# Two heads in turn in the third layer's half-array products, with one ring of six PSUM banks

## The chip, the core and the metric

The kernel runs on one core of a Trainium2 chip. The metric is the device time of one execution in microseconds (us); the time before is the median of three runs.

## The reference, cut to what matters

Three layers work in turn on 512 tokens of width 1024: a gated delta-rule layer, a stick-breaking attention layer, and a third layer with two branches and a mixture of experts ("PEER"). All is float32. The change concerns two stages of the third layer, and an ordering in the second. The third layer's windowed attention has 16 query heads of 64 dimensions, 2 key and value heads, blocks of 128 queries that each see their own block and the one before, and a sink logit a head:

```python
s = jnp.einsum('bqhgd,bkhd->bhgqk', qj, kj) * scale
s = jnp.where(valid, s, -jnp.inf)
m = jnp.maximum(jnp.max(s, axis=-1, keepdims=True), sink)
p = jnp.exp(s - m)
denom = jnp.sum(p, axis=-1, keepdims=True) + jnp.exp(sink - m)
return jnp.einsum('bhgqk,bkhd->bqhgd', (p / denom), vj)
```

Its second branch is a matrix-memory recurrence (mLSTM) of 8 heads with keys of 64 and values of 128 dimensions; within a block it needs the scores `einsum('bhtd,bhsd->bhts', qj, kj) * w_intra`.

## The kernel before, in words

TensorE (PE) does all products; a product is a weight load (the stationary operand) and a matmul that streams the other operand past it. Activations and weights of the projections are split into a high and a low part, so that three one-pass products stand for one (`mm3`, lines 104 to 108); the attention's own products are plain float32, and the trace shows each of them as two records. A head has 64 dimensions, so two heads lie in the two halves of the 128 partitions. Their score products use 64 rows of the array, their value products 64 columns of it.

The program is written in one order of source lines. A scheduler then places the instructions on the engines' queues: on each engine it takes what is ready by its own timing, earlier source lines first as a rule, so that projections of later steps fill the time in which PE would wait. Nothing is pinned by hand in the stages that change, apart from the dependences. PSUM has eight banks; two serve projections (`pj`), the other six are shared out by tags (`psum`, `pg`).

`window_pair` (lines 877 to 931) does one pair of heads in the third layer, 8 calls, each in two steps (`t2`) of two query blocks. For each head `e` it writes the mask into a bank of tag `l` by a product with the identity (line 895, full array, 256 columns) and adds the scores (line 896, 64 rows, 256 columns, 128 for the first block), block after block, so that full-array and half-array products alternate. VectorE (DVE) takes the maximum (898), ScalarE (ACT) the exponential with its sum (906), DVE scales (916), PE transposes into the bank `pt` (918), DVE or ACT copies (922), and PE multiplies with the values (928, 64 columns) into the bank `x`, first all of head 0, then all of head 1. Banks: three `l`, one each `x`, `t` (the transposes of the query norm, line 713) and `pt`.

`mlstm_pair` (lines 1001 to 1085), 4 calls, makes for each of two heads the decay matrix `W` (1030, 1032) and the scores (1035, four products of 64 rows and 128 columns) and multiplies them (1037). Its banks are two `w`, three `num`, one `pc`.

`sb_pair` (lines 775 to 820) is the second layer's attention, 8 calls. There the source lists scores (790) and value products (819) with the two heads in turn already, on six banks of one tag.

Of the kernel before, what the change touches and what calls it, by code (L numbers as in the profile page):

```python
# [2 lines left out]

# [1 line left out]

# [5 lines left out]
F32 = mybir.dt.float32  # L11
# [4 lines left out]
AF = mybir.ActivationFunctionType  # L16
ALU = mybir.AluOpType
AX = mybir.AxisListType

P = 128  # L20
# [3 lines left out]
NT = T // P  # L24
# [9 lines left out]
class Net:  # L34
# [185 lines left out]
        self.split(H[:, k], L[:, k], n, eb=nc.gpsimd if k % 2 else nc.vector)  # L220


    def wtile(self, w, j0, n=2, ks=slice(0, KC)):


        nc = self.nc
        self.uid += 1
        raws = []
        for j in range(n):
            raw = self.wr.tile([P, KC, P], F32, tag="raw", name=f"wr{self.uid}_{j}")  # L230
            nc.sync.dma_start(raw[:, ks], w[j0 + j][:, ks])
            raws.append(raw)
        parts = {}

        def at(k):
            f = k // self.part
            if f not in parts:
                fs = slice(max(f * self.part, ks.start), min((f + 1) * self.part, ks.stop))
                wh = self.ws.tile([P, self.blocks, self.part, P], F32R, tag="wh", name=f"wh{self.uid}")
                wl = self.ws.tile([P, self.blocks, self.part, P], F32R, tag="wl", name=f"wl{self.uid}")  # L240
                o = slice(fs.start - f * self.part, fs.stop - f * self.part)
                for j, raw in enumerate(raws):
                    self.split(wh[:, j, o], wl[:, j, o], raw[:, fs], eb=nc.gpsimd if self.uid % 9 else nc.vector)
                parts[f] = wh, wl
            wh, wl = parts[f]
            return wh[:, :n, k % self.part], wl[:, :n, k % self.part]
        return at
# [79 lines left out]
class Gdn(Net):  # L327
    SPARE_SB, SPARE_2, SPARE_P = "pj pj l l", "pj pj l l", "pj pj s s"
    RAW, SB_, PART = 3, 3, 2
    FIRST, OFF, A0, WB, SPARE_0, SQ = (0, 8, 16), (), 12, 6, "v0", 8  # L330
    SP = 5
    YB = 8
    EARLY_A, EARLY_OUT = (slice(0, 7), slice(7, 8)), (slice(0, 6), slice(6, 8))
    RATE, LV = 1.0, 100
# [342 lines left out]
class Sb(Gdn):  # L677
# [97 lines left out]
    def sb_pair(self, wk, j, kT, qT, v, idr, sbm, nui, nones):  # L775


        nc = self.nc
        mm = nc.tensor.matmul
        half = [slice(e * 64, e * 64 + 64) for e in range(2)]  # L780

        names = ("b0", "b1", "c0", "c1", "a0", "a1")
        bank = {n: self.pg()[:, :256 if n < "d" and n > "c" else T] for n in names}

        def reg(t, e, b):
            o = 384 if b == 3 else 0
            return t[f"{'abcb'[b]}{e}"][:, o:o + (NT - b) * P]
        order = [(e, b) for b in (1, 3, 2, 0) for e in range(2)]
        for e, b in order:
            mm(reg(bank, e, b), kT[half[e], b * P:(b + 1) * P], qT[half[e], b * P:],  # L790
               start=b != 3, stop=False, skip_group_check=True)
        for e, b in order:
            mm(reg(bank, e, b)[:, :P], idr, sbm, start=False, stop=True, skip_group_check=True)
        sH, sL, wt = {}, {}, {}
# [9 lines left out]
        for n in names:  # L804
            e = int(n[1])
# [7 lines left out]
                            bufs=2 if n[0] == "c" else self.SP)  # L813
            nc.scalar.activation(wt[n], bank[n], AF.Exp)
        po = self.pg()
        for b in range(NT):
            for e in range(2):
                h = 2 * j + e
                mm(po[half[e], b * P:], v[:, b, h * 64:(h + 1) * 64], reg(wt, e, b), start=b == 0, stop=b == NT - 1)
        return po  # L820


# [4 lines left out]
class Second(Sb):  # L827
# [49 lines left out]
    def window_pair(self, wk, j, qT, kTx, v, wmask, idr, aH, aL):  # L877

        nc = self.nc
        mm = nc.tensor.matmul  # L880
        kv = j // 4
        po = self.pg("x")
        sink = self.col("sink", 2 * j, 2).unsqueeze(1).to_broadcast([P, 2, 2])
        for t2 in range(0, NT, 2):
            small = lambda n: wk.tile([P, 2, 2], F32, tag=n, name=f"{n}{j}_{t2}", bufs=3)
            mx, den, sm = small("mx"), small("den"), small("sm")
            lg = []
            for e in range(2):
                L = self.pg("l").rearrange("p (i s) -> p i s", i=2)
                lg.append(L)  # L890
                pr = slice(e * 64, e * 64 + 64)
                for i in range(2):
                    tb = t2 + i
                    n = P if tb == 0 else 2 * P
                    mm(L[:, i], idr, wmask[tb > 0], start=True, stop=False)
                    mm(L[:, i, 2 * P - n:], qT[pr, tb * P:(tb + 1) * P], kTx[e == kv][pr, (tb + 1) * P - n:(tb + 1) * P],
                       start=False, stop=True)
                nc.vector.tensor_reduce(mx[:, :, e], L, axis=AX.X, op=ALU.max)
            nc.vector.tensor_tensor(mx, mx, sink, op=ALU.max)
            nc.vector.tensor_tensor(den, sink, mx, op=ALU.subtract)  # L900
            nc.vector.tensor_scalar(mx, mx, -1.0, None, op0=ALU.mult)
# [4 lines left out]
                    nc.scalar.activation(Pm[e][:, i], lg[e][:, i], AF.Exp, bias=mx[:, i, e:e + 1], accum_out=sm[:, i, e:e + 1])  # L906
            nc.vector.tensor_tensor(den, den, sm, op=ALU.add)
            nc.vector.reciprocal(den, den)
            for e in range(2):
                pr = slice(e * 64, e * 64 + 64)  # L910
                pT = self.pg("pt")
                k = 0
                for i in range(2):
                    n = min(t2 + i + 1, 2)
                    x = Pm[e][:, i, (2 - n) * P:]
                    nc.vector.tensor_scalar(x, x, den[:, i, e:e + 1], None, op0=ALU.mult)
                    for b in range(n):
                        nc.tensor.transpose(pT[:, k * P:(k + 1) * P], x[:, b * P:(b + 1) * P], self.ident)
                        k += 1
                PT = wk.tile([P, 4, P], F32, tag="PT", name=f"PT{j}_{e}_{t2}")  # L920
                ev = nc.scalar.copy if e else nc.vector.tensor_copy
                ev(PT[:, :k], pT[:, :k * P].rearrange("p (k t) -> p k t", t=P))
                k = 0
                for i in range(2):
                    tb = t2 + i
                    n = min(tb + 1, 2)
                    for b in range(n):
                        mm(po[pr, tb * P:(tb + 1) * P], v[:, tb + 1 - n + b, kv * 64:kv * 64 + 64], PT[:, k],
                           start=b == 0, stop=b == n - 1)
                        k += 1  # L930
        self.split(aH[:, j], aL[:, j], po)

# [68 lines left out]
    def mlstm_pair(self, wk, j, qT, kT, mv, gcol, rr, selp, dcm, mo, hH, hL):  # L1001

        nc = self.nc
# [14 lines left out]
        for i in range(NT):  # L1018
# [1 line left out]
        kw = new("mkw", [NT, 2, 64])  # L1020
        nc.vector.tensor_tensor(kw, p.rearrange("p (i e d) -> p i e d", i=NT, e=2),
                                gcol[:, 1, :, 2 * j:2 * j + 2].unsqueeze(3).to_broadcast([P, NT, 2, 64]), op=ALU.mult)
        PT = {}
        for e in range(2):
            h = 2 * j + e
            pr = slice(e * 64, e * 64 + 64)
            pm = self.rep(h, rr)
            W = new("mW", [NT, P])
            for i in range(NT):
                nc.vector.scalar_tensor_tensor(W[:, i], pm[:, i * P:(i + 1) * P], gcol[:, 0, i, h:h + 1], dcm,  # L1030
                                               op0=ALU.add, op1=ALU.add)
            nc.scalar.activation(W, W, AF.Exp)
            p = self.pg()
            for i in range(NT):
                mm(p[:, i * P:(i + 1) * P], kT[pr, i * P:(i + 1) * P], qT[pr, i * P:(i + 1) * P], start=True, stop=True)
            PT[e] = new("mPT", [NT, P], 3)
            nc.vector.tensor_tensor(PT[e], v4(p), W, op=ALU.mult)

        num = [self.pg("num")[:, :3 * (P + 1)].rearrange("p (g c) -> p g c", c=P + 1) for _ in range(3)]
        at = lambda i, e: num[(2 * i + e) // 3][:, (2 * i + e) % 3]  # L1040
# [46 lines left out]
    def second(self, x):  # L1087
        nc, tc, a = self.nc, self.tc, self.a
        w = a["w_in"]
        with ExitStack() as st:  # L1090
# [18 lines left out]
                self.proj_T(w, 10 + j2, 2, act, lambda j, p: keep("mq", j2 + j, p, 1.0))  # L1109
                self.proj_T(w, 14 + j2, 2, act, lambda j, p: keep("mk", j2 + j, p, 0.125))  # L1110
            with ExitStack() as s1:
                self.TT = "t"
                self.psum(s1, l=3, x=1, t=1, pt=1)
                wk = s1.enter_context(tc.tile_pool(name="c_wk", bufs=2))
                c1 = s1.enter_context(tc.tile_pool(name="c_c1", bufs=1))
                idr, wp, wc = self.load_const(c1, ("id", "wp", "wc"), F32R)
# [523 lines left out]
```

## Time and profile before

| | |
|---|---|
| median of three runs | 2853.34 us (2845.3 to 2853.7) |
| the profiled execution | 2852.8 us, span 2851.0 us |
| PE busy | 2671.3 us, 94% of the span |
| DVE busy | 1786.9 us, 63% |
| ACT busy | 1210.9 us, 42% |
| POOL busy | 1765.5 us, 62% |
| mean granted TensorE clock | 0.98 |

The span is the time from the first to the last instruction of the profiled execution, and its own time lies just around it. Engines run beside each other, so their shares don't add up. PE is the matmul stream, PEld its weight loads. Matmuls are pipelined: a record's duration reaches over the start of the next one, and what a product costs is read from one start to the next. In the rows below, `64*128 64x256` is a product that uses 64 rows and 128 columns of the array and streams 256 columns; `x8` joins eight records.

### The profile page before, as it was taken

To read this page: it belongs to the slowest core of one execution; us is meant where nothing else is said; L and a number is where in the kernel's file an instruction comes from. 1 tells how busy PE (TensorE), PEld (TensorE's weight loads), DVE (VectorE), ACT (ScalarE), POOL (GpSimd) and SP (SyncE) were. 2 spreads that over 40 slices of the span, in tenths; PEclk is the share of its full clock that TensorE was granted. 3 is DMA by queue.
4 is the path that set the end of the run, shared out by engine and by line. 5 is a ranking of instruction groups with operands and counts; after the bars stand their busy time and mean duration, and the time that the engine had idled before them with its cause. 6 is when DMAs were issued, how large, how long until landed. Compare 5 with 4: busy or idle time off the path is not lost. (4 is left out here: it accounts for less than half of the span.)

```text
span 2851.0 us, 40457 instructions
## 1 busy us (share of the span) xinstructions
PE 2671.3 (94%) x14601; PEld 2266.0 (79%) x14601; DVE 1786.9 (63%) x3095; ACT 1210.9 (42%) x2508; POOL 1765.5 (62%) x1335
## 2 busy tenths in 40 slices
PE   6999898799998999999998989998998999999999
PEld 4877777697776877778786988898998978877777
DVE  7767664614446654122332989899899166778886
ACT  5566663636654454233333333333333333333332
POOL 4889883533333522433463468788788378888786
PEclk9999999899998999999999999999999999999999
DMA  6334331221011111221222587887987879999996
GB/s 240 108 119 125 111 113 31 76 90 60 31 39 54 56 45 60 74 69 66 69 79 89 160 296 261 284 290 256 314 277 281 276 272 344 340 333 331 333 328 227
DMA packets 206793, 499.35 MB, mean 175 GB/s; under 512 B 18304, under 2 KB 106624, under 8 KB 203520
## 3 DMA queue, kind: packets, MB, share of 16 engines
q1 hardware_dynamic: 167856, 359.19, 37.6%
q0 software_dynamic: 36864, 134.23, 13.1%
q10 hardware_dynamic: 1872, 3.33, 0.4%
q8 instruction: 115, 1.88, 0.3%
q14 instruction: 86, 0.70, 0.1%
HBM read 444.26 MB, written 52.43 MB: 174 GB/s over the span
## 5 line engine op out<-in xcount | busy, mean ns | idle before, releaser
L102 POOL TENSOR_TENSOR wl<-wr,wh 128x256 fp32r<-128x256 f32 (+2 forms) x499 | 414.8, 850 | 499.2 <-ACT wh L99 468.5
L102 POOL TENSOR_TENSOR upl<-upr,uph 128x1024 fp32r<-128x1024 f32 x128 | 312.9, 2445 | 97.0 <-ACT uph L99 96.3
L99 ACT ACTIVATE wh<-wr 128x256 fp32r<-128x256 f32 (+2 forms) x556 | 228.7, 445 | 302.6 <-PE pj L107 120.4
L106 PE MATMUL pj<-nH,downh 128*128 128x384 f32 x1024 | 354.3, 346 | 2.3 <-ACT w L1459 1.7
L108 PE MATMUL pj<-nH,downl 128*128 128x384 f32 x1024 | 349.6, 341 | 4.6 <-DVE downl L102 4.6
L107 PE MATMUL pj<-nL,downh 128*128 128x384 f32 x1024 | 348.8, 341 | 0.0
L102 POOL TENSOR_TENSOR downl<-downr,downh 128x1024 fp32r<-128x1024 f32 x96 | 243.9, 2542 | 129.3 <-ACT downh L99 126.4
L1504 PE MATMUL acc<-uph,wwh 128*128 128x512 f32 x768 | 302.7, 399 | 6.9 <-ACT wwh L99 6.9
L1504 PE MATMUL acc<-upl,wwh 128*128 128x512 f32 x768 | 305.4, 398 | 0.0
L99 ACT ACTIVATE downh<-downr 128x1024 fp32r<-128x1024 f32 x128 | 135.4, 1059 | 307.0 <-PE pj L107 163.2
L102 DVE TENSOR_TENSOR wwl<-wo,wwh 128x384 fp32r<-128x384 f32 x128 | 196.1, 1533 | 76.4 <-ACT wwh L99 70.5
L1504 PE MATMUL acc<-uph,wwl 128*128 128x512 f32 x768 | 232.4, 398 | 6.6 <-DVE wwl L102 6.5
L108 PE MATMUL pj<-hH,wl 128*128 128x512 f32 x544 | 222.8, 411 | 0.9 <-POOL wl L102 0.8
L106 PE MATMUL pj<-hH,wh 128*128 128x512 f32 x544 | 220.5, 405 | 2.1 <-ACT mo L1175 1.1
L107 PE MATMUL pj<-hL,wh 128*128 128x512 f32 x544 | 215.8, 397 | 0.0
L99 ACT ACTIVATE uph<-upr 128x1024 fp32r<-128x1024 f32 x128 | 134.8, 1053 | 174.9 <-POOL upl L102 116.1
L106 PEld LDWEIGHTS pj<-nH,downh 128*128 128x128 f32 x1024 | 193.7, 189 | 6.6 <-ACT w L1459 2.0
L108 PEld LDWEIGHTS pj<-nH,downl 128*128 128x128 f32 x1024 | 193.3, 189 | 5.3 <-DVE downl L102 4.9
L107 PEld LDWEIGHTS pj<-nL,downh 128*128 128x128 f32 x1024 | 193.6, 189 | 0.0
L1428 POOL DMA_INDIRECT gdown<-in_peer_down,idx x128 | 165.7, 1295 | 44.3 <-issue 13.7
L1504 PEld LDWEIGHTS acc<-uph,wwh 128*128 128x128 f32 x768 | 145.6, 190 | 44.6 <-ACT wwh L99 9.4
L1504 PEld LDWEIGHTS acc<-uph,wwl 128*128 128x128 f32 x768 | 144.8, 189 | 43.4 <-DVE wwl L102 8.3
(621 smaller groups left out, 6702.2 us busy)
## 6 DMA issues: line engine op xcount, KB each, us to landing
downr<-in_peer_down_j SPq DMA_DIRECT2D x128, 512.0 KB, 4.8
upr<-in_peer_up_j SPq DMA_DIRECT2D x128, 512.0 KB, 6.3
wr<-in_w_in SPq DMA_DIRECT2D x50, 512.0 KB, 4.2
ada<-in_w_ada SPq DMA_DIRECT2D x48, 512.0 KB, 3.7
wait<-w SPq DMA_DIRECT2D x128, 192.0 KB, 4.9
wo<-wait SPq DMA_DIRECT2D x128, 192.0 KB, 5.2
G<-stage SPq DMA_DIRECT2D x24, 1024.0 KB, 6.9
Gt<-G SPq DMA_DIRECT2D x48, 512.0 KB, 8.0
```

The source lines that it names most:

```text
L99: nc.scalar.activation(h, src, AF.Copy)
L102: return (eb or nc.vector).tensor_tensor(l, src, h.bitcast(F32), op=ALU.subtract)
L106: mm(out, lh, rh, start=start, stop=False)
L107: mm(out, lh, rl, start=False, stop=False)
L108: mm(out, ll, rh, start=False, stop=stop)
L1428: nc.gpsimd.indirect_dma_start(out=g, out_offset=None, in_=self.a[f"peer_{name}"], in_offset=bass.IndirectOffsetOnAxis(ap=self.idx[:, s:s ...
L1504: mm(po[z][b], lh[:, zs], rh[:, bs], start=False, stop=j == P - 1 and rh is uh and lh is l, skip_group_check=True)
```

## The change

A helper `in_order` is new: it chains all PE instructions that are traced inside it in the order of the source, without a semaphore; other instructions may still come between them. It is put around the score and the value products of `sb_pair`, whose source order stays. In `window_pair` the masks of both heads come first, then the scores block by block with the two heads in turn; the transposes of both heads, then the value products with the heads in turn. All its banks, and those of the query norm's transposes, are of the one tag `l` with six banks, and the transposed weights `PT` have four buffers in place of two. In `mlstm_pair` the decay matrices of both heads come first, then the scores with the heads in turn.

```diff
+    @contextmanager
+    def in_order(self):
+
+        tc, bb = self.tc, self.nc.cur_bb.bb
+        n = len(bb.instructions)
+        yield
+        last = None
+        for i in list(bb.instructions)[n:]:
+            if i.engine == mybir.EngineType.PE:
+                if last is not None:
+                    tc.add_manual_dep(i, last.name, mybir.DependencyInfo(
+                        mybir.DependencyClass.NoSync, mybir.DependencyReason.DATA), reason="in_order")
+                last = i
...
+    PTB = 4
...
-        for e, b in order:
-            mm(reg(bank, e, b), kT[half[e], b * P:(b + 1) * P], qT[half[e], b * P:],
-               start=b != 3, stop=False, skip_group_check=True)
+        with self.in_order():
+            for e, b in order:
+                mm(reg(bank, e, b), kT[half[e], b * P:(b + 1) * P], qT[half[e], b * P:],
+                   start=b != 3, stop=False, skip_group_check=True)
...
-        for b in range(NT):
-            for e in range(2):
-                h = 2 * j + e
-                mm(po[half[e], b * P:], v[:, b, h * 64:(h + 1) * 64], reg(wt, e, b), start=b == 0, stop=b == NT - 1)
+        with self.in_order():
+            for b in range(NT):
+                for e in range(2):
+                    h = 2 * j + e
+                    mm(po[half[e], b * P:], v[:, b, h * 64:(h + 1) * 64], reg(wt, e, b), start=b == 0, stop=b == NT - 1)
...
-        po = self.pg("x")
+        po = self.pg("l")
...
-            lg = []
-            for e in range(2):
-                L = self.pg("l").rearrange("p (i s) -> p i s", i=2)
-                lg.append(L)
-                pr = slice(e * 64, e * 64 + 64)
+            lg = [self.pg("l").rearrange("p (i s) -> p i s", i=2) for e in range(2)]
+            with self.in_order():
+                for e in range(2):
+                    for i in range(2):
+                        mm(lg[e][:, i], idr, wmask[t2 + i > 0], start=i == 0, stop=False, skip_group_check=True)
                 for i in range(2):
                     tb = t2 + i
                     n = P if tb == 0 else 2 * P
-                    mm(L[:, i], idr, wmask[tb > 0], start=True, stop=False)
-                    mm(L[:, i, 2 * P - n:], qT[pr, tb * P:(tb + 1) * P], kTx[e == kv][pr, (tb + 1) * P - n:(tb + 1) * P],
-                       start=False, stop=True)
-                nc.vector.tensor_reduce(mx[:, :, e], L, axis=AX.X, op=ALU.max)
+                    for e in range(2):
+                        pr = slice(e * 64, e * 64 + 64)
+                        mm(lg[e][:, i, 2 * P - n:], qT[pr, tb * P:(tb + 1) * P], kTx[e == kv][pr, (tb + 1) * P - n:(tb + 1) * P],
+                           start=False, stop=i == 1, skip_group_check=True)
+            for e in range(2):
+                nc.vector.tensor_reduce(mx[:, :, e], lg[e], axis=AX.X, op=ALU.max)
...
+            PT = []
             for e in range(2):
-                pr = slice(e * 64, e * 64 + 64)
-                pT = self.pg("pt")
+                pT = self.pg("l")
...
-                PT = wk.tile([P, 4, P], F32, tag="PT", name=f"PT{j}_{e}_{t2}")
+                PT.append(wk.tile([P, 4, P], F32, tag="PT", name=f"PT{j}_{e}_{t2}", bufs=self.PTB))
                 ev = nc.scalar.copy if e else nc.vector.tensor_copy
-                ev(PT[:, :k], pT[:, :k * P].rearrange("p (k t) -> p k t", t=P))
-                k = 0
+                ev(PT[e][:, :k], pT[:, :k * P].rearrange("p (k t) -> p k t", t=P))
+            k = 0
+            with self.in_order():
                 for i in range(2):
                     tb = t2 + i
                     n = min(tb + 1, 2)
                     for b in range(n):
-                        mm(po[pr, tb * P:(tb + 1) * P], v[:, tb + 1 - n + b, kv * 64:kv * 64 + 64], PT[:, k],
-                           start=b == 0, stop=b == n - 1)
+                        for e in range(2):
+                            mm(po[e * 64:e * 64 + 64, tb * P:(tb + 1) * P], v[:, tb + 1 - n + b, kv * 64:kv * 64 + 64], PT[e][:, k],
+                               start=b == 0, stop=b == n - 1)
                         k += 1
...
-            nc.scalar.activation(W, W, AF.Exp)
-            p = self.pg()
+            nc.scalar.activation(W[e], W[e], AF.Exp)
+        p = [self.pg() for e in range(2)]
+        with self.in_order():
             for i in range(NT):
-                mm(p[:, i * P:(i + 1) * P], kT[pr, i * P:(i + 1) * P], qT[pr, i * P:(i + 1) * P], start=True, stop=True)
+                for e in range(2):
+                    pr = slice(e * 64, e * 64 + 64)
+                    mm(p[e][:, i * P:(i + 1) * P], kT[pr, i * P:(i + 1) * P], qT[pr, i * P:(i + 1) * P], start=True, stop=True)
+        for e in range(2):
             PT[e] = new("mPT", [NT, P], 3)
-            nc.vector.tensor_tensor(PT[e], v4(p), W, op=ALU.mult)
+            nc.vector.tensor_tensor(PT[e], v4(p[e]), W[e], op=ALU.mult)
...
-                self.TT = "t"
-                self.psum(s1, l=3, x=1, t=1, pt=1)
+                self.TT = "l"
+                self.psum(s1, l=6)
```

## Rows read from the trace of the kernel before

**Rows 1.** The page, part 1: PE's busy time, share and instructions.
```profile
PE 2671.3 (94%) x14601; PEld 2266.0 (79%) x14601; DVE 1786.9 (63%) x3095; ACT 1210.9 (42%) x2508; POOL 1765.5 (62%) x1335
```

**Rows 2.** Busy time by stretch: the window's attention and the mLSTM.
```profile
core 0: us, PE busy (x) PEld busy (x) DVE busy (x) ACT busy (x) POOL busy (x), PEclk, DMA share, GB/s
...
920.00:1160.00 240.00, 236.38 (x1336) 180.06 (x1335) 124.32 (x337) 105.98 (x309) 88.25 (x112) 1.00 0.16 53
...
1210.00:1420.00 210.00, 207.15 (x1198) 163.51 (x1197) 51.16 (x127) 70.98 (x224) 84.00 (x116) 1.00 0.19 66
```

**Rows 3.** PE's longest wait, 920 to 1170 us: total, times, longest, us.
```profile
PE x L928 <- DVE PT L922: 0.8, 1, 0.8
```

**Rows 4.** Timeline 1000 to 1010 us, PE: start, us, engine, line, operation.
```profile
1001.72 0.28 PE L106 MATMUL pj<-wh,hH 128*128 128x256 f32 x1
...
1001.84 0.28 PE L107 MATMUL pj<-wl,hH 128*128 128x256 f32 x1
...
1002.04 1.09 PE L928 MATMUL x<-PT,v 128*64 128x128 f32 x8
...
1003.06 0.55 PE L918 MATMUL pt<-c_id,Pm 128*128 128x128 f32 x3
...
1003.37 0.36 PE L895 MATMUL l<-wmask,cr_id 128*128 128x256 f32 x1
...
1004.39 0.70 PE L896 MATMUL l<-kTs,qT 64*128 64x256 f32 x2
...
1005.01 0.39 PE L108 MATMUL pj<-wh,hL 128*128 128x256 f32 x1
...
1005.23 0.28 PE L106 MATMUL pj<-wh,hH 128*128 128x256 f32 x1
...
1005.35 0.28 PE L895 MATMUL l<-wmask,cr_id 128*128 128x256 f32 x1
...
1007.12 0.38 PE L107 MATMUL pj<-wl,hH 128*128 128x256 f32 x1
```

**Rows 5.** Line 928, value products: durations ns, first and last start us, forms.
```profile
L928 PE MATMUL x<-PT,v x224: 272/273/324, 963.0 to 1156.7; 128*64 128x128 f32 x112
```

**Rows 6.** Timeline of PE, second layer's scores, 656 to 664 us.
```profile
656.19 2.43 PE L790 MATMUL l<-q,kT 64*128 64x384 f32 x16
658.55 1.11 PE L793 MATMUL l<-cr_sbm,cr_id 128*128 128x128 f32 x8
```

**Rows 7.** Timeline of PE, second layer's value products, 680 to 687 us.
```profile
680.47 1.07 PE L819 MATMUL l<-wta,v 128*64 128x512 f32 x2
681.47 0.92 PE L790 MATMUL l<-q,kT 64*128 64x384 f32 x4
682.32 0.64 PE L819 MATMUL l<-wta,v 128*64 128x512 f32 x1
...
684.62 1.78 PE L790 MATMUL l<-q,kT 64*128 64x128 f32 x10
```

**Rows 8.** Lines 898, 906 and 922: ns min/median/max of DVE and ACT.
```profile
L898 DVE TENSOR_REDUCE mx<-l x32: 670/691/693, 948.8 to 1124.7; 128x2 f32<-128x512 f32 x32
...
L922 DVE COPY PT<-pt x16: 545/615/692, 960.1 to 1152.7; 128x384 f32<-128x384 f32 x8, 128x512 f32<-128x512 f32 x8
L922 ACT COPY PT<-pt x16: 472/536/588, 964.4 to 1155.3; 128x384 f32<-128x384 f32 x8, 128x512 f32<-128x512 f32 x8
...
L906 ACT ACTIVATE Pm<-l,mx x64: 458/476/504, 952.1 to 1137.3; 128x256 f32<-128x256 f32 x64
L906 ACT ACTIVATION_READ_ACCUMULATOR Pm<-l,mx x64: 192/205/236, 952.4 to 1137.7; 128x1 f32 x64
```

**Rows 9.** Timeline of PE, mLSTM scores of one head, 1215 to 1217 us.
```profile
1215.32 1.16 PE L1035 MATMUL w<-mq,mk 64*128 64x128 f32 x8
1216.40 0.44 PE L1054 MATMUL pc<-mv,mkw 64*64 64x129 f32 x4
```

**Rows 10.** PE's longest wait, second layer, 600 to 920 us.
```profile
PE l L811 <- DVE sHa_a L101: 2.0, 2, 1.7
```

More of the change, by code (lines that the diff above doesn't have):

```diff
@@ L1 @@
 import math
-from contextlib import ExitStack
+from contextlib import ExitStack, contextmanager
 import numpy as np
@@ L1022, in mlstm_pair @@
                                 gcol[:, 1, :, 2 * j:2 * j + 2].unsqueeze(3).to_broadcast([P, NT, 2, 64]), op=ALU.mult)
-        PT = {}
+        PT, W = {}, {}
         for e in range(2):
             h = 2 * j + e
-            pr = slice(e * 64, e * 64 + 64)
             pm = self.rep(h, rr)
-            W = new("mW", [NT, P])
+            W[e] = new("mW", [NT, P])
             for i in range(NT):
-                nc.vector.scalar_tensor_tensor(W[:, i], pm[:, i * P:(i + 1) * P], gcol[:, 0, i, h:h + 1], dcm,
+                nc.vector.scalar_tensor_tensor(W[e][:, i], pm[:, i * P:(i + 1) * P], gcol[:, 0, i, h:h + 1], dcm,
                                                op0=ALU.add, op1=ALU.add)
-            nc.scalar.activation(W, W, AF.Exp)
-            p = self.pg()
+            nc.scalar.activation(W[e], W[e], AF.Exp)
+        p = [self.pg() for e in range(2)]
+        with self.in_order():
             for i in range(NT):
-                mm(p[:, i * P:(i + 1) * P], kT[pr, i * P:(i + 1) * P], qT[pr, i * P:(i + 1) * P], start=True, stop=True)
+                for e in range(2):
+                    pr = slice(e * 64, e * 64 + 64)
+                    mm(p[e][:, i * P:(i + 1) * P], kT[pr, i * P:(i + 1) * P], qT[pr, i * P:(i + 1) * P], start=True, stop=True)
+        for e in range(2):
             PT[e] = new("mPT", [NT, P], 3)
-            nc.vector.tensor_tensor(PT[e], v4(p), W, op=ALU.mult)
+            nc.vector.tensor_tensor(PT[e], v4(p[e]), W[e], op=ALU.mult)
         num = [self.pg("num")[:, :3 * (P + 1)].rearrange("p (g c) -> p g c", c=P + 1) for _ in range(3)]
```

## The prediction

> **What bounds the kernel now.** I read the page of the profile first, then the busy time by stretch, the PE waits of the stretch that changes, and last its timeline, one product after another. The page shows PE busy for 94% of the span [rows 1]. That is an average over stages, so I looked at the stretches that the change touches [rows 2]: the windowed attention with the projections laid between its steps (920 to 1160 us) has PE busy for 236.4 of 240 us at a granted clock of 1.00, the matrix-memory (mLSTM) stretch 207.2 of 210. DVE is busy for 124 us of the first and ACT for 106, so neither is near a bound. The longest wait of PE on another engine in the attention is 0.8 us [rows 3]. PE it is, and a microsecond taken from PE there is a microsecond off the end, as long as PE finds other work.
>
> But busy is not the same as streaming. In the timeline [rows 4] the reader should look at the distance from one start to the next, not at the durations. Full-array products of 256 columns start 0.12 us apart (1001.72, 1001.84). A mask product has the same 256 columns. One head's scores in the first half-sequence, two masks and two products of 64 rows, take 1.64 us (1003.37 to 1005.01); in the second half 1.77 us (1005.35 to 1007.12). The 64-row product of 256 columns at 1004.39 holds PE until 1005.01, 0.62 us. A float32 product stands in the trace as two records: the 112 value products of the source are x224 [rows 5].
>
> The second layer shows the same 64-row products with two heads in turn: 16 records, that is 8 products, 1280 columns a head, from 656.19 to 658.55, 2.36 us [rows 6]. A single value product of 512 columns took 1.00 us (680.47 to 681.47) [rows 7]; 1280 columns at that rate, 2.5 us, would be the time of one head alone. So the two heads ran beside each other. For products of 64 columns: between 682.32 and 684.62 PE did fourteen records, one head's 512, 384, 256 and 128 and the other's 384, 256 and 128 [rows 7]. 2048 columns in turn would need 4.0 us at the rate of the single product; they took 2.30. Two column halves overlap as well.
>
> What a change between full array and half array costs follows from the same timeline [rows 4]. The 256-column product takes 0.62 us, while the pure stream at the second layer's rate is (2.36 - 0.19) / 1280 = 1.70 ns a column, 0.43 us; so 0.19 us goes into the entry and exit that lie inside the run. Another 0.09 us goes on the record before (1001.84 to 1002.04 is 0.20 where 0.12 is usual) and 0.1 on the one after (1005.01 to 1005.23 is 0.22).
>
> **The change, part by part.** No instruction, byte or DMA is added or removed; none is moved past the queues of SP or POOL. What moves is the order on PE and the banks.
>
> *Scores of the window.* Eight pairs, two halves each, 16 steps. Before: a step costs two heads of 1.64 or 1.77, plus 0.1 after each: 3.48 or 3.74 us. After: four masks at 0.12 (0.48), 0.09 on the way in, the paired stream of 384 or 512 columns at 1.70 ns (0.65 or 0.87), 0.19 inside the run and 0.1 behind: 1.51 or 1.73. The step saves 1.97 or 2.01; times 8 each, **31.8 us**. Most of it is the changes of shape (four a step become one), the rest the overlap.
>
> *Value products of the window.* Before: four products of one head from 1002.04 to 1003.06 [rows 4], 1.02, with 0.09 before and an estimated 0.06 behind 1.17 us; three products three quarters of the stream (0.87 of the 1.02), 0.95. Both heads double that. If a step's run stays whole, both heads cost what one did: 8 x 1.17 + 8 x 0.95 = 17.0 us. But the first head's product can go as soon as its own copy is done; the second head's follows a copy on another engine (DVE 0.62, ACT 0.54 [rows 8]) behind transposes that come later. In the second layer, whose source writes the heads in turn too, the first head's first product runs alone at 680.47 and the others two microseconds later [rows 7]. Pinning an order does not forbid projections in between. I assume the same here for all 16: each lone product costs its own 0.22 and a second run's 0.30, 8.3 us. That leaves **8.7 us**; the ends are 8.7 and 17.0, and I take the lower since the nearest row shows it.
>
> *mLSTM scores.* Four products of one head take 1.08 us (1215.32 to 1216.40) [rows 9], with 0.1 on the record before 1.18. Four pairs of heads, one of two runs saved: **4.7 us**. The second head's bank now comes free only after both row broadcasts are read; the projections queued there cover that (PE 207 of 210 us [rows 2]). Without that cover it would cost a read of four DVE operations a pair, some 1.1 us, four times.
>
> *Second layer, order pinned.* The trace shows nearly the pinned order already [rows 6, 7]. I take 0. Lower end: a product that waits for its partner, one wait like the 1.7 us there [rows 10] per pair, 13 us lost; upper end: the lone first product joins the others, 1.0 us x 8 gained.
>
> *One ring of six banks, four buffers for the transposed weights.* The value accumulator, scores, transposes and the transposes of the q norm share what were banks 3, 1, 1 and 1. The second head's transposes no longer wait for the copy of the first. On PE that is worth nothing by itself, since projections fill the wait; without them, one copy (0.6 us) a step. What is late next: with less PE work between the steps, PE meets the chain reduction, exponentials, scaling, copy earlier. I charge 0.3 us a step for it, 5 us, between nothing and 1.7 us a step [rows 10].
>
> Sum: 31.8 + 8.7 + 4.7 - 5 = 40 us. The profiled execution took 2852.8 us (span 2851.0), 0.5 below the median of the three runs, so the sum stands against 2853 either way: **2813 us**.
>
> One thing could take a little back. Had the second head started one record late, the second layer's run would be 0.32 us longer (a 384-column record at 0.85 us for two of 512), 2.68 in place of 2.36 [rows 6]. Were the records taken in strict order here, the first of every run would stand alone: 16 score runs at 0.11 or 0.21 us, 16 value runs and 4 of the mLSTM at 0.11, together 5 us, and the time 2818. I give that 0.1, inside the forecast's share. The Trainium skill, "TensorE: Matmul & The Clock Gate", section Part 3: Packing small matmuls, does say that matmuls are never reordered, start and end in program order. By that rule the second layer's first records would not be beside each other; the 2.36 us speaks against it, or for a program order that already alternates.
>
> **The rivals.**
> *The steps, not PE, set the pace.* The 32 value runs go from 963.0 to 1156.7 [rows 5], 12.1 us a step. Were that spacing the chain's own, PE would use up its projections early and then idle: no change, 2853. For it: the spacing is even. Against it: reduction 2 x 0.69, exponentials 4 x (0.48 + 0.20), copy 0.62 [rows 8] and 3 us of PE are some 8 us, 128 us for 16 steps in strict sequence, and more banks let steps overlap. DVE with 124 of 240 us [rows 2] is no limit either. Chance 0.08. The Trainium skill, "TensorEngine Tiling (Array Packing)", section PSUM Bottleneck, warns of this case: once the array is packed, copies out of PSUM may be the limit.
>
> *It does not do what it says*: heads stay in turn on paper, but projections fall between them, so that little overlaps. Then only the shape changes go: three of four in a step, 48 x 0.38 = 18 us, less 5: 2840. The second layer's overlap speaks against it [rows 6, 7]. Chance 0.08.
>
> *Slower.* The pinned scores need two free banks at once, in a ring that also holds the accumulator, two transposes and the q norm's. PE takes its queue in order; if it stands at the second head's mask until the last step's exponentials (2.7 us) and what precedes them are through, projections behind it stand too. At 4 us a step it is 64 us against the 45 saved: 2872. It decides from 2.8 us a step. Against it: five of six banks cover a whole step, and the waits now are under 1 us [rows 3]. Chance 0.07.
>
> *More than forecast*: value runs stay whole and nothing waits, 31.8 + 17.0 + 4.7 = 53.5: 2799. Chance 0.25.
>
> **How the numbers follow.** The forecast has 0.52, its own range 2805 to 2828 (waits between 0 and 1 us a step more than charged). The range 2796 to 2840 holds forecast, more and part of the poor overlap, with the run-to-run spread below; outside are the pace of the chain, the slower case and some of the tails. A measurement tells about 0.3% (8.6 us) from no change. Faster by more: 0.52 + 0.25 + 0.08, a little over for partial mixes, 0.86. Within: 0.07. Slower: 0.07.
>
> **What would show it.** Right: 64-row window products starting in pairs a few ns apart, one run a step; runs of score products falling from about 1.7 us a head to under 1.3 for both; the stretch up to the first branch projection about 35 us shorter; DVE and ACT busy time unchanged. Lone value products first in a run: my assumption of 8.3 us; whole runs: the larger gain. Wrong: PE waits on ACT or DVE of more than 10 us in the attention, a granted clock below 1.00 there, or score runs still one head at a time.

## The result and the profile after

The changed kernel took 2872.7 us (median of 12 runs, 2861.65 to 2888.61), the kernel before beside it 2854.6 (12 runs). The ratio is 1.006, 95% interval 1.0039 to 1.0081: **slower by 0.6%**, where 2813 was forecast. The profiled execution took 2870.6 us, its span is 2868.8.

Part 1 of the page of the changed kernel answers to [rows 1]:

```profile
PE 2649.7 (92%) x14601; PEld 2257.9 (79%) x14601; DVE 1787.5 (62%) x3095; ACT 1211.5 (42%) x2508; POOL 1762.0 (61%) x1335
```

PE has 22 us less to do, as hoped, and the span is 18 us longer; PE now waits. Busy time by stretch of the changed kernel: the attention from the third layer's first product to its last value product, two stretches inside it, and the mLSTM (compare [rows 2]):

```profile
core 0: us, PE busy (x) PEld busy (x) DVE busy (x) ACT busy (x) POOL busy (x), PEclk, DMA share, GB/s
890.00:1173.00 283.00, 232.54 (x1425) 189.05 (x1426) 135.53 (x373) 113.90 (x322) 94.25 (x115) 0.88 0.15 50
980.00:1000.00 20.00, 14.95 (x96) 11.98 (x97) 10.85 (x27) 7.01 (x22) 5.62 (x4) 0.74 0.01 2
1020.00:1040.00 20.00, 11.79 (x60) 7.58 (x59) 8.77 (x25) 6.76 (x25) 2.82 (x4) 0.70 0.08 32
1225.00:1430.00 205.00, 202.90 (x1204) 161.68 (x1204) 51.32 (x123) 70.55 (x220) 85.22 (x117) 1.00 0.20 67
```

The mLSTM is as full as before. In the attention PE stands for 50 of 283 us, and the granted clock there is 0.88. PE's waits of that stretch (total, times, longest) name what it stands for, where [rows 3] had 0.8:

```profile
PE l L938 <- DVE Pm L936: 23.1, 8, 4.1
PE l L1011 <- DVE mix L983: 7.6, 1, 7.6
...
PE l L729 <- POOL rv_ak L123: 3.8, 1, 3.8
```

Line 938 transposes the weights and waits for DVE's scaling (936); line 1011 transposes the mLSTM's gate rows into columns and waits for those rows. PE's timeline, line by line, shows what the change did and what it cost:

```profile
648.72 2.43 PE L807 MATMUL l<-q,kT 64*128 64x384 f32 x16
...
960.80 0.43 PE L950 MATMUL l<-PT,v 128*64 128x128 f32 x2
961.16 0.39 PE L909 MATMUL l<-wmask,cr_id 128*128 128x256 f32 x1
961.48 0.87 PE L950 MATMUL l<-PT,v 128*64 128x128 f32 x10
962.28 0.62 PE L909 MATMUL l<-wmask,cr_id 128*128 128x256 f32 x3
962.82 0.48 PE L915 MATMUL l<-kT,qT 64*128 64x256 f32 x1
962.83 0.48 PE L915 MATMUL l<-kTs,qT 64*128 64x256 f32 x1
963.14 0.38 PE L915 MATMUL l<-kT,qT 64*128 64x256 f32 x1
963.15 0.38 PE L915 MATMUL l<-kTs,qT 64*128 64x256 f32 x1
963.36 0.38 PE L915 MATMUL l<-kT,qT 64*128 64x256 f32 x1
...
963.58 0.38 PE L915 MATMUL l<-kT,qT 64*128 64x256 f32 x1
...
970.89 1.03 PE L938 MATMUL l<-c_id,Pm 128*128 128x128 f32 x6 [0.73 <-DVE Pm L936]
971.67 0.71 PE L909 MATMUL l<-wmask,cr_id 128*128 128x256 f32 x4
...
974.29 1.09 PE L950 MATMUL l<-PT,v 128*64 128x128 f32 x14 [0.31 <-ACT PT L942]
978.69 1.07 PE L938 MATMUL l<-c_id,Pm 128*128 128x128 f32 x6 [3.31 <-DVE Pm L936]
979.95 0.58 PE L950 MATMUL l<-PT,v 128*64 128x128 f32 x2 [0.19 <-DVE PT L942]
980.46 1.22 PE L909 MATMUL l<-wmask,cr_id 128*128 128x256 f32 x4
...
982.20 0.63 PE L915 MATMUL l<-kT,qT 64*128 64x256 f32 x1
...
982.63 0.63 PE L915 MATMUL l<-kT,qT 64*128 64x256 f32 x1
...
988.56 1.51 PE L938 MATMUL l<-c_id,Pm 128*128 128x128 f32 x6 [4.09 <-DVE Pm L936]
989.86 1.91 PE L729 MATMUL l<-c_id,nsq_aq 128*128 128x128 f32 x8
...
996.76 0.39 PE L106 MATMUL pj<-wh,hH 128*128 128x256 f32 x1 [0.96 <-DVE nsq_aq L711]
...
1240.49 1.16 PE L1059 MATMUL w<-mq,mk 64*128 64x128 f32 x14
```

Scores of the two heads start 10 ns apart (962.82, 962.83): they run beside each other. But between 970 and 990 the reader sees one step after another: transposes (938), then the next step's masks (909) and scores, values (950), and then PE waits 3.31 or 4.09 us for the next weights, with no projection in between.

To see where the time went I put, for the attention stretch, each interval from one PE start to the next to the kind of the first record, and PE's waits apart. "Scores ahead" counts the steps, of 15, whose scores come on PE before the transposes of the step before. In us:

| | before | changed | ring alone | in turn, old banks | the same, whole runs |
|---|---|---|---|---|---|
| stretch | 259 | 283 | 313 | 229 | 224 |
| PE waits | 9.4 | 50.9 | 40.1 | 14.5 | 14.9 |
| masks and scores | 53.7 | 32.8 | 62.6 | 27.5 | 27.8 |
| transposed weights | 12.1 | 16.7 | 15.8 | 13.9 | 12.6 |
| values | 29.2 | 22.2 | 33.8 | 20.6 | 14.9 |
| all other PE work | 155.7 | 161.5 | 161.2 | 153.5 | 155.0 |
| granted clock | 0.97 | 0.88 | 0.86 | 0.97 | 0.96 |
| scores ahead | 14 | 0 | 0 | 15 | 15 |

(The last three columns are experiments, below.) Before to changed: waits +41.5, scores -20.9, values -7.0, and the transposes and other work, unchanged in number, 10.4 dearer (the last section says why): +24. The stretch from the last attention branch projection to the first product of the mLSTM's output fell from 217 to 212. What lies before the attention differs by up to 17 us between the profiled executions (it starts at 888 to 905 us), which is why stretches are compared here, and medians for the whole.

### The profile page after: what moved, and what is told of

It is laid out like the page before. It is cut to its first block, busy times and chain, and to the rows that moved or that the text cites. A ratio compares the mean times of both kernels' runs of the same rounds, so it can differ in the third digit from the quotient of the medians.

```text
span 2868.8 us, 40480 instructions
## 1 busy us (share of the span) xinstructions
PE 2649.7 (92%) x14601; PEld 2257.9 (79%) x14601; DVE 1787.5 (62%) x3095; ACT 1211.5 (42%) x2508; POOL 1762.0 (61%) x1335
## 5 line engine op out<-in xcount | busy, mean ns | idle before, releaser
L1529 PEld LDWEIGHTS acc<-uph,wwl 128*128 128x128 f32 x768 | 144.6, 189 | 45.2 <-DVE wwl L102 10.3
```

What stands on the lines that cost most here:

```text
L1529: mm(po[z][b], lh[:, zs], rh[:, bs], start=False, stop=j == P - 1 and rh is uh and lh is l, skip_group_check=True)
```

## The experiments

The expectations call the theories by letters. A blames the shared ring, B the two heads at once; A2 the place of the gate rows, A3 and A4 the ring's order. A5, the last, says that the order of first writes in the source counts, the accumulator's included. Each ratio is to the kernel before run beside it, whose median lay between 2854.6 and 2860.7 us; times of different experiments compare to within some 6 us, ratios better.

**The query norm's bank.** The changed kernel with the query norm's transposes on a bank of their own.

```diff
-                self.TT = "l"
-                self.psum(s1, l=6)
+                self.TT = "t"
+                self.psum(s1, l=5, t=1)
```

> The changed kernel, but the transposes of the query norm get a bank of their own again (five for the attention, one for them). Theory A, the shared ring: in the changed kernel these transposes stand in line behind all tiles of the pairs before them (30 to 57 us after their input), so the next projections find no free buffer and PE has nothing to do beside the softmax chain. With their own bank they follow their input within 10 us, PE's waits on DVE line 936 fall from 23 us to under 6, and the time is 2805 to 2830. Theory B, the pinned two-head groups bring both heads' softmax at once and expose the chain whatever the banks: waits of 15 us and more stay, time 2855 to 2875.

2863.2 us, ratio 1.0032 (1.0012 to 1.0051). PE's waits fall from 51 to 41 us, scores ahead stay at 0. The interval just overlaps that of the changed kernel, so the gain is seen in the waits. A part of it, no more.

**The ring alone.** The kernel before, heads in sequence, nothing pinned, its mLSTM as it was; only the banks of the change.

```diff
-        po = self.pg("x")
+        po = self.pg("l")
...
-                pT = self.pg("pt")
+                pT = self.pg("l")
...
-                self.TT = "t"
-                self.psum(s1, l=3, x=1, t=1, pt=1)
+                self.TT = "l"
+                self.psum(s1, l=6)
```

> The kernel before with the one ring of six alone; heads one after the other, nothing pinned. Theory A: the transposes of the query norm come late here too, PE idles, and without the saving of the heads in turn it is the slowest of all: 2870 to 2910. Theory B: the ring by itself costs nothing, 2845 to 2860.

2903.6 us, ratio 1.0163 (1.0135 to 1.019). The ring by itself costs 47 us (2903.6 less 2856.4 beside it). Its attention by stretch and PE's waits there show the signature of the changed kernel, with the old order of heads:

```profile
896.00:1209.00 313.00, 273.34 (x1426) 210.63 (x1426) 135.50 (x373) 114.30 (x322) 93.77 (x115) 0.86 0.13 46
```

```profile
PE l L918 <- DVE Pm L916: 16.7, 7, 3.4
PE l L989 <- DVE mix L961: 7.6, 1, 7.6
```

**The turn on the old banks.** The changed kernel with the six banks shared out as before.

```diff
-        po = self.pg("l")
+        po = self.pg("x")
...
-                pT = self.pg("l")
+                pT = self.pg("pt")
...
-                self.TT = "l"
-                self.psum(s1, l=6)
+                self.TT = "t"
+                self.psum(s1, l=3, x=1, t=1, pt=1)
```

> The changed kernel on the banks of before (three, one, one, one). Theory A: 2805 to 2835; the second head's transposes wait for the copy of the first again, which projections cover. Theory B: 2855 to 2880, as the changed kernel or worse.

2825.3 us, ratio 0.9884 (0.9864 to 0.9904): faster by 1.2%. Its attention by stretch, and PE's timeline over one step:

```profile
900.00:1129.00 229.00, 215.23 (x1426) 175.19 (x1426) 140.06 (x372) 112.73 (x322) 94.83 (x115) 0.97 0.19 62
```

```profile
979.18 1.09 PE L950 MATMUL x<-PT,v 128*64 128x128 f32 x14
980.20 0.55 PE L938 MATMUL pt<-c_id,Pm 128*128 128x128 f32 x3
980.50 0.36 PE L106 MATMUL pj<-wh,hH 128*128 128x256 f32 x1
...
982.71 0.39 PE L909 MATMUL l<-wmask,cr_id 128*128 128x256 f32 x2
983.03 0.37 PE L915 MATMUL l<-kT,qT 64*128 64x128 f32 x1
983.04 0.37 PE L915 MATMUL l<-kTs,qT 64*128 64x128 f32 x1
...
986.25 0.43 PE L950 MATMUL x<-PT,v 128*64 128x128 f32 x2
986.61 0.38 PE L107 MATMUL pj<-wl,hH 128*128 128x256 f32 x1
```

Now transposes, scores and values of different steps stand among projections, and nothing waits there. The scores of a step run 17.9 us ahead of its transposes on average (28.5 before, 8.8 in the changed kernel), so its maxima, exponentials and scaling are done when PE comes to it.

**No order pinned** in the window, on the ring (both pins of `window_pair` gone).

```diff
-            with self.in_order():
+            if True:
```

> The changed kernel without the pins in the window's attention; order of the source and ring of six stay. Theory A: the pins are not the cause, 2860 to 2885. Theory B: the scheduler is free to stagger the heads, the time falls to 2850 or below.

2878.5 us, ratio 1.0059 (1.0038 to 1.008): no difference to the changed kernel; PE waits 50.7 us. The pins are not what costs.

**Two tenants out of the ring.** Of the kinds of tile that share the ring two go: query norm and gate rows share one bank, the rest has five (`t=1` stands first and so is the default).

```diff
-                self.TT = "l"
-                self.psum(s1, l=6)
+                self.TT = "t"
+                self.psum(s1, t=1, l=5)
```

> As the first experiment (attention on a ring of five), but the bank of its own serves the transposes of the query norm and the gate rows. Theory A2, the gate rows: on the attention's ring they wait for their turn behind the fourth pair, and the gate projections, PE's filler, wait for them since both use the same tile; here they come earlier, PE has its filler back between 1000 and 1050 us, and the time falls to 2825 to 2845. Theory A3, the ring's order serializes the steps themselves (a step's scores wait for the banks of the one before), whatever the filler: 2855 to 2870, as the first experiment.

2850.0 us, ratio 0.9966 (0.9945 to 0.9988). PE waits 31.7 us, scores ahead still 0. Against the first experiment (1.0032) only the gate rows and the few other tiles without a tag of their own have moved, and the wait for the gates falls from 7.6 to 1.6 us: on the ring their place does cost.

**Gate rows earlier** in the source, on the ring of six.

```diff
-                    if j2 == 2:
+                    if j2 == 0:
```

> The changed kernel, ring of six and all, with the gate rows called after the second pair in place of the fourth. Theory A2: the gate projections can start some 60 us earlier, the wait of 7.6 us on them goes, and the time falls by 15 to 35 us, to 2835 to 2860. Theory A3: 2865 to 2880.

2879.3 us, ratio 1.007 (1.0035 to 1.0105); PE waits 50.7 us. A miss: called earlier, but still on the ring, they gain nothing, and their wait of 7.6 us stays.

**Whole value runs**, on the old banks: in each pair of products the head whose copy ends later comes first, so that none goes alone. The edit is made to the kernel of the third experiment.

```diff
-                        for e in range(2):
+                        for e in (1, 0):
```

> The heads in turn on the banks of before (2825 us), the value products beginning with the second head, whose copy is the later one. If the lone first product (2 records ahead of each run) costs what the prediction charged, 16 x 0.52, the runs are whole, two records fewer stand alone a step, and the time is 2815 to 2820. If PE is not the bound there any more, or the first head's copy is then the later one, 2823 to 2832.

2819.0 us, ratio 0.9863 (0.9829 to 0.9897), the lowest median of all. Its interval overlaps that of the third experiment, so the gain of this order alone is read from the traces: 229 to 224 us in the stretch. PE's timeline at one step:

```profile
975.13 1.09 PE L950 MATMUL x<-PT,v 128*64 128x128 f32 x16
976.16 0.55 PE L938 MATMUL pt<-c_id,Pm 128*128 128x128 f32 x3
```

Both heads' sixteen records take 1.03 us, what one head's eight took in [rows 4]; the value run is whole in all 16 steps.

**Two banks for the transposes, two for the scores**, otherwise the third experiment.

```diff
-                self.psum(s1, l=3, x=1, t=1, pt=1)
+                self.psum(s1, l=2, x=1, t=1, pt=2)
```

> The heads in turn with two banks for scores (and gate rows), one for the accumulator, one for the query norm, two for the transposes. If the overlap of one step's scores with the last step's softmax is what matters, two score banks give it away: 2840 to 2860. If only the kinds must not stand in one line, it is 2820 to 2832, like three and one.

2828.2 us in one run, scores ahead 13 of 15. By this one run even two banks for the scores are enough, with only the gate rows beside them in the tag. PE waits 7.3 us for the gates here too.

**The transposed weights' bank.** The changed kernel with those on a bank of their own, ring of five.

```diff
-                pT = self.pg("l")
+                pT = self.pg("pt")
...
-                self.psum(s1, l=6)
+                self.psum(s1, l=5, pt=1)
```

> The changed kernel with the transposes of the weights alone taken off the ring (one bank for them, five for all the rest). Theory A4, banks are dealt in the order of the source: on one ring the next step's score banks stand behind this step's transposes, so PE has a step's scores at the earliest behind the transposes of the one before (0 of 15 steps overlap in the changed kernel, 15 of 15 on the banks of before). With the transposes off the line most steps overlap again, PE's waits on DVE line 936 go under 5 us, and the time is 2825 to 2845. If the query norm's place in the line is the larger part, 2850 to 2865.

2861.8 us, ratio 1.0033 (1.0016 to 1.0051). Scores ahead 6 of 15. Again only part.

**Scores of both halves first.** Ring of six and all its tenants; only the source order changes: a pair's scores are written for both halves before the first half's maxima.

```diff
+        banks = {}
         for t2 in range(0, NT, 2):
...
+            banks[t2] = lg
+        for t2 in range(0, NT, 2):
+            lg = banks[t2]
```

> The ring of six kept, but the source asks for the scores of both halves of a pair before the first softmax. Theory A4: within a pair the second step's scores stand ahead of the first one's transposes, 7 or 8 of 15 steps overlap, and the time falls to 2835 to 2860. If it is the number of banks and not their order: 2865 to 2885, as the changed kernel.

2835.4 us, ratio 0.9921 (0.9896 to 0.9947). With no bank more, 37 us come back. Scores ahead 8 of 15, one in each pair. In PE's waits those for the scaled weights have left the top of the list; the one for the gates is still there:

```profile
PE l L1015 <- DVE mix L987: 7.6, 1, 7.6
```

**No pins anywhere**, on the kernel with whole runs (all five uses of `in_order`).

```diff
-            with self.in_order():
+            if True:
```

> The fastest so far (banks of before, heads in turn, second head's value product first, 2819 us) without any pin. If the pins are needed for the overlap of the heads, score runs break up and the time rises by 5 to 20 us; if the order of the source is enough, 2815 to 2825.

2835.0 us, ratio 0.9925 (0.9904 to 0.9945). PE's timeline shows whose loss it is:

```profile
971.38 0.51 PE L909 MATMUL l<-wmask,cr_id 128*128 128x256 f32 x2 [0.40 <-ACT Pm L926]
971.82 1.13 PE L915 MATMUL l<-kTs,qT 64*128 64x256 f32 x4
...
973.35 0.40 PE L909 MATMUL l<-wmask,cr_id 128*128 128x256 f32 x2
973.67 0.92 PE L915 MATMUL l<-kT,qT 64*128 64x128 f32 x4
```

Without the pin the scores go one head at a time again, in 14 of 16 steps: masks and scores cost 40.5 us in place of 27.8. The value runs stay whole without it. On banks that let steps overlap the five pins are worth some 16 us, 12 of them in this stretch.

**Both tenants out.** Query norm and transposed weights each on a bank of their own, ring of four.

```diff
-                pT = self.pg("l")
+                pT = self.pg("pt")
...
-                self.TT = "l"
-                self.psum(s1, l=6)
+                self.TT = "t"
+                self.psum(s1, l=4, t=1, pt=1)
```

> The changed kernel with two kinds taken out of the ring at once: the transposes of the weights and those of the query norm each have a bank of their own, scores, accumulator and gate rows keep a ring of four. Either move alone gave some 10 us (the weights' transposes 2861.75, the query norm's 2863.2). A4 (whatever stands in one tag stands in line behind this step's transposes, so each move alone only hands the place in the queue to the next): together they give far more than the sum of both, 2825 to 2840, near the 2825.3 of the banks of before, and the next step's scores are ahead of this step's transposes in 13 or more of 15 steps. If the two losses simply add, 2850 to 2856 (2872.7 less 10 less 11). If the accumulator or the gate rows in the ring are what is left: above 2845, with the wait of the gate rows for their gates (7.6 us) still there.

2856.4 us, ratio 1.0002 (0.9981 to 1.0023): the mere sum, a miss for A4. Its timeline shows who is left in the line:

```profile
1002.28 0.55 PE L938 MATMUL pt<-c_id,Pm 128*128 128x128 f32 x3 [0.65 <-DVE PT L942]
1002.76 0.43 PE L950 MATMUL l<-PT,v 128*64 128x128 f32 x2
1003.12 0.74 PE L909 MATMUL l<-wmask,cr_id 128*128 128x256 f32 x4
```

The masks of a pair's second half (909) follow at once on the first value product of its first half (950), which opens the accumulator's bank. Scores ahead 6 of 15. In the traces of all sixteen kernels PE first writes the tiles of one tag in the order in which their source first writes them, without one exception (in the ring of six, the 72 tiles of the window's steps, with those of the query norm and the gate rows between them). So the accumulator stands in line where its first product stands, behind the transposes and ahead of the next scores.

**The accumulator's bank** taken out, the transposes left in.

```diff
-        po = self.pg("l")
+        po = self.pg("x")
...
-                self.TT = "l"
-                self.psum(s1, l=6)
+                self.TT = "t"
+                self.psum(s1, l=4, x=1, t=1)
```

> The changed kernel with the query norm on a bank of its own, as in the first experiment (2863.2), and the value accumulator on one too; scores, the weights' transposes and the gate rows keep a ring of four. A5 (the tiles of one tag are first written in the order of the source; the next step's scores stand behind this step's transposes, and a pair's second half behind the accumulator's first product as well): the transposes are still ahead in the line, so the next scores come before this step's transposes in none of 15 steps, and the time stays at 2852 to 2868. With the transposes taken out as well it is the run on the banks of before, 2825.3. If the accumulator that holds a bank for a whole pair were the cost by itself: 2825 to 2842.

2843.9 us, ratio 0.9961 (0.9939 to 0.9983): between the two ranges. Scores ahead of the transposes 0 of 15, as A5 says, but ahead of the first value product 14 of 15 (4 in the changed kernel), and that alone gains more than A5 allowed. With the query norm on its own bank, the square against the kernel before reads 1.0032 (neither out), 1.0002 (transposes out), 0.9961 (accumulator out), 0.9884 (both).

**Each step's scores first.** Ring of six again, the scores of every step of a group of two pairs written ahead of the rest of the step before (`scores` and `rest` are the two parts of `window_pair`'s step).

```diff
-                        self.window_pair(wk, j, q[j], {True: kT, False: kTs}, v, wmask, idr, aH, aL)
+                        for scores, rest, t2 in self.window_pair(wk, j, q[j], {True: kT, False: kTs}, v, wmask, idr, aH, aL):
+                            scores(t2)
+                            if late:
+                                late()
+                            late = lambda rest=rest, t2=t2: rest(t2)
+                    late()
```

> The changed kernel, ring of six and all its tenants as they are; in the source the scores of each step of a group of two pairs are written ahead of the step before's maxima, transposes and value products (4 steps a group, so 12 of the 15 passages). A5: only the line counts, so the next step's scores come ahead of this step's transposes in 12 or more of 15 steps, PE's idle time in the attention falls below the 23.8 us of the run that did so for the two halves of one pair (2835.4), and the time is 2818 to 2840. If too few banks were the cost, the line changes nothing more: 2845 or above, with PE waiting at the masks for exponentials.

2840.1 us, ratio 0.9936 (0.9914 to 0.9959), at the edge of A5's range; scores ahead 12 of 15 as foretold. PE's waits, 30.3 us, are not below the 23.8 of the two halves, so the further passages gained nothing. PE still waits 7.6 us for the gates, 5.2 for the scaling and 3.7 for the key norm; what those cost at the end was not tried.

## Why the prediction was wrong

**The step that failed** is "One ring of six banks, four buffers for the transposed weights", charged at "0.3 us a step for it, 5 us, between nothing and 1.7 us a step". It cost 47 us: 2903.6 against 2856.4 with the ring alone, 2872.7 against 2825.3 with the heads in turn (which keeps the four buffers). I counted free banks ("five of six banks cover a whole step"). Banks were not short: on the same six, the order of the source alone gave 37 us back. What one tag shares is a line. Its tiles are first written in the order of the source, and there the next step's scores stand behind this step's transposes and the accumulator's first product. Before, with tags apart, scores ran ahead in 14 of 15 steps; on the ring in none. A step then takes 14.7 us from scores to last value product with the next right behind it, where before several steps of 40.4 us lay over each other, 12.7 us from one step's first value product to the next. Between the parts of one step PE has only projections to do, and these stand behind the query norm's transposes, which are in the same line (above: the transposes at 989.86 free the norm's buffer, and the projection at 996.76 then waits until DVE has read `nsq_aq` out of the projections' bank). The 0.8 us of [rows 3] was read as room; it was the result of the overlap that the change took away.

**PE as the bound**: right before, and the sentence "as long as PE finds other work" held the risk. It finds none in 51 us of the changed attention.

**Scores, 31.8 us**: right in kind, somewhat too large. On the old banks masks and scores fall by 26.2 us, and the other work, which carries the neighbours' part, by 2.2. In the changed kernel 20.9, since part of it runs at the lower clock: there the 50 mask and score records cost 12.4 us where at the higher level 142 cost 20.3. The 5 us that strict order might have cost did not come: the first scores of the two heads start within 10 ns in all 16 steps. (That side sum took 0.85 us for two records of 512 columns; [rows 7] has 1.00. The forecast does not use it.)

**Value products, 8.7 us**: 8.6 on the old banks, with the lone first product that was assumed (986.25 there) in 15 of 16 steps. The larger end, 17.0, asked for whole runs: with them 14.3 are saved.

**mLSTM, 4.7 us**: 217 to 212, and 217 with the ring alone, which has no such edit. But most of it is lost right behind: in all 14 kernels with the edit the projection that follows takes 56.0 to 57.5 us from its first to its last product, where it took 52.5 before and 52.7 with the ring alone. Eight records slip behind its first product, and PE waits 3.3 us in place of 1.2 for the last heads' output. Over both stretches it is 268.0 us against 269.6, a gain of 1.6. **Second layer, 0**: its sixteen score records take 2.43 us as in [rows 6].

**The sum without the ring**: 45 us were counted. On the old banks scores and neighbours give 28.4, value products 8.6, the mLSTM 1.6, while PE's waits cost 5.1 more and the transposes 1.8. That makes 31.7; the medians differ by 31.1 (2856.4 less 2825.3).

**Pins** were given no worth of their own in the window. On the ring they have none, the scores stand in pairs without them; on the old banks all five are worth 16 us, 12 of them in the window's stretch.

**The rivals.** The slower rival gave 2872, the time that came, at a chance of 0.07. That the number fits is luck, for its place was wrong: PE was to stand at the second head's mask for want of a bank, but line 909 leads no wait of note; PE stands at the transposes, for DVE's scaling. "The steps, not PE, set the pace" was closer in mechanism than in its terms: 12.1 us a step was no limit (10.3 on the old banks, counted the same way), the ring made the steps the limit. The Trainium skill, "TensorEngine Tiling (Array Packing)", section PSUM Bottleneck, warns that copies out of PSUM may be the next limit; here DVE was busy for 136 of 283 us, and the order in which banks are handed out was the limit, not the copying.

**What would show it**: DVE's and ACT's busy time did not change and scores came in pairs, both as forecast; the first value product went alone in 11 of 16 steps. The stretch up to the first branch projection, which was to be some 35 us shorter, went from 241 to 245 us (212 on the old banks). Two of the signs named for a wrong forecast came: waits of over 10 us on DVE (23.1) and a clock below 1.00.

Not settled: the 10 us between the ring with scores first (2835.4) and the old banks (2825.3). The gate rows' wait of 7.6 us need not be it: with two banks for the scores PE waited 7.3 us for the gates as well, and that one run took 2828.2.

## What to carry to other kernels

Before tiles are put on one PSUM tag, write down the order in which the source first writes them, and ask which later step now overlaps an earlier one: one tag is one line, and what fills the gaps (here the query norm) must not stand in it. A stretch in which PE never waits may owe that to steps lying over each other; look how far ahead of its consumer each product runs before calling the short waits room. Where products of half the array are to run in pairs, look whether they do, pin them where they don't (here the scores), and let the operand that comes last go first (here the value products); that, on separate banks, was the 1.4% that beat both kernels.

## What had not been expected of the hardware

Waits of 3 to 4 us cost more than themselves. In the changed attention 68 of 283 us ran at the lower of the two clock levels (1.2 GHz), where it was 15 of 259 before and 15 of 229 on the old banks; those 15 lie at the start of the stretch in all three, the other 53 around the later places at which PE stood. The same product can be read at either level in the timeline of the changed kernel above. A pair of score records takes 0.22 us at 963.36, 0.43 at 982.20, behind the wait of 3.31 us. A transpose record costs 110 ns at the higher level and 238 at the lower, a record of the other PE work 169 and 265; before, at the higher level, they cost 108 and 170. By these records the 10.4 us of unchanged work are the clock's. The Trainium skill, "TensorE: Matmul & The Clock Gate", section "A second HAM failure mode: psum-queue depth-cycling", tells of a kernel that cycles through PSUM banks and idles a little between groups of products, so that its clock swings between the two levels; this trace agrees in the swing, with 0.70 to 0.74 granted in the stretches above, though its waits are of 3 to 4 us.
